# Fifth stage of a hybrid decoder step: one plain group of heads instead of two, with the second group's weight sums formed there

## The chip, the cores and the metric

The kernel is one launch on one core of a Trainium2 chip. The metric is the device time of that core in microseconds; the median of three runs of the kernel before is 2309.34 us (2308.86 to 2309.92). All data are fp32 in the device's main memory.

## The reference, cut to what matters

One step of a small decoder: a pooling mixer (layer A), one shared K/V projection, and a layer B of sliding-window attention with sinks, each closed by a layer norm. 1024 prompt tokens and 8 samples of one token pass through, so 1032 columns in all.

```python
def attn_layer(x, pos, kb, vb, k_pos, q_pos, blocked, w_in, sinks, w_out, g_ln, b_ln):
    B, T, _ = x.shape
    z = x @ w_in
    q = rope_partial(z[..., :D_ATTN].reshape(B, T, N_HEADS, HEAD_DIM), pos)
    gate = z[..., D_ATTN:]
    ...
    o = attn_core(q, kb, vb, q_pos, k_pos, sinks).reshape(B, T, D_ATTN)
    y = (o * jax.nn.silu(gate)) @ w_out
    return layer_norm(ALPHA * x + y, g_ln, b_ln)

def reference(...):
    ...
            xp, sp = pool_layer(xp, prefix_p, pos_p, w_in_a[i], ...)
            xs, ss = pool_layer(xs, state_pool[i], pos_s, w_in_a[i], ...)
            k_p, v_p = shared_kv(xp, pos_p, w_kv)
            ...
            xp = attn_layer(xp, pos_p, kb_p, vb_p, ..., w_in_b[j], sinks_b[j], w_out_b[j], ...)
            xs = attn_layer(xs, pos_s, kx_s, vx_s, ..., w_in_b[j], sinks_b[j], w_out_b[j], ...)
```

Here `x @ w_in`, `x @ w_kv` and the two `@ w_out` are the large products: 2048 deep, 2048 or 4096 wide (the K/V one 512).

## The kernel before

**Tiles.** The tokens are cut into two chunks, c = 0 with 512 columns and c = 1 with 520. Each large product is made as weights (128 by 128 blocks, held) times activations (columns stream). An fp32 operand is split into a high part (a cast, done by ScalarE) and a low part (the rest, a subtraction done by VectorE), and a product is three matmuls: high by high, high by low, low by high. A weight block set of 128 rows by 1024 columns is prepared by one load (L285, on the queue of SyncE), one cast (L505, ScalarE) and one subtraction (L520, VectorE). Activation tiles are prepared the same way by a load (L828), a cast (L838) and a subtraction (L847); `x_begin(nxt)` opens that work for the next phase, one small step with each tick of the program.

**Stages and phases.** There are eight stages: input product of layer A for c = 0 and c = 1, its output product for both, then the same for layer B: `bi` (K, V, queries, gates, attention) for c = 0, the fifth stage, and c = 1, the sixth, and `bo` (output product) for both. The tuple `PHASES` lists them. The stages that begin on fresh activations, the first and the fifth, are cut into two phases, a plain one (`PLAIN`) and one that uses a seven-product scheme.

- *Plain* (`unit`, L698): one result tile of 128 rows by 512 columns is 48 matmuls of 512 columns (16 blocks times three; L712, L713, L714) into one PSUM bank, closed by one ScalarE copy (L2127, L2135, L2140). A unit has four ticks. In the fifth stage the plain phase has `part` (0, 2): four units for K and V (two each), then for each of the two groups p four units (query and gate tiles of t = 2p and 2p + 1), twelve in all.
- *Seven-product* (`seven`, L596): a pair of result tiles is made by seven products instead of eight on halves of the token columns, 24 matmuls each of 256 (c = 1: 260) columns (L684, L685, L686), 168 in all for what 96 matmuls of 512 columns make in the plain form. It needs seven prepared weight operands instead of four plain blocks, and after each product a ScalarE or VectorE step on the bank (L623 to L657).

**Weight sums.** Four of the seven operands are sums of weight blocks. `first_pair` (L335) loads the blocks, forms the four sums on VectorE (L349) and, with `keep`, stores each of them (512 KB) by a DMA from GpSimd's queue (L351), so that the next stage's `next_pair` only loads them. Where the plain phase has used the blocks without sums (`bare_pair`), nothing is stored, and the sixth stage forms them itself with `first_pair(..., False)`. The tuple `FORM` = (0, 1) names the groups for which this is so.

**Banks.** `psD` (L242) hands out three PSUM banks in a ring, one a unit. The seven-product scheme uses the same three banks by a table of its own (L604), in which two of them change roles from pair to pair (`flip`). A product that is given a bank has to wait until the step that reads the bank's earlier content is done.

**Order.** `in_order` (L85) fixes the order of each engine's instructions as the source writes them. What an engine does next is therefore settled when the program is built: events at ticks (`at`), the small steps of `x_tick`, and a side job whose steps are taken one a tick. During the plain phase of the fifth stage the side job is the layer norm of chunk 1 (`ln_gen(1)`: VectorE L974, L1037, L1071, L895 to L898; ScalarE L1060), and the attention of the first heads runs too (VectorE L1899, L1903, L1921, L1922; ScalarE L1914, L1927).

The next phase's activations are opened inside the loop over t, for groups 0 and 1 at t = 1, between its query unit and its gate unit, five units before the end of the plain phase:

```python
                self.unit(q_done)
                if t == 2 * ps[-1] - 1:
                    self.x_begin(nxt)
                self.last = t == 2 * ps[-1] + 1
                self.unit(g_done)
```

Of the kernel before, what the change touches and what calls it, by code (L numbers as in the profile page):

```python
# [47 lines left out]
N_CST = K_MP + P + 1  # L48

PHASES = (  # L50
    ("ai", 0, (0, 1)), ("ai", 0, (1, 8)), ("ai", 1, (0, 8)), ("ao", 0, None), ("ao", 1, None), ("bi", 0, (0, 2)),
    ("bi", 0, (2, 8)), ("bi", 1, (0, 8)), ("bo", 0, None), ("bo", 1, None),
)
PHASE_OF = {"x": "ai", "g": "ao", "h": "bi", "o": "bo"}
INPUT_OF = {k: x for x, k in PHASE_OF.items()}
# [15 lines left out]
)  # L71

LATE = (2, 3)
FORM = (0, 1)
X_KEEP = 5
X_AGE = 3
SIDE_KEEP = 5
# [113 lines left out]
class Kern:  # L191
# [185 lines left out]
    def build_stream(self):  # L377
        io = self.io
        w = []
        for kind, c, part in PHASES:  # L380
# [18 lines left out]
            elif kind == "bi":  # L399
                if part[0] == 0:  # L400
                    w += self.next_pairs("wkv", range(2), locked) if seven else pr("wkv", 0) + pr("wkv", 1)
                if seven:
                    for p in range(*part):
                        for q in (p, 8 + p):
                            if c == 1 and p in FORM:
                                f = self.first_pair("wib", q, False)
# [3 lines left out]
                else:  # L410
                    for p in range(*part):
                        q, g = ((self.bare_pair if p in FORM else pr)("wib", q) for q in (p, 8 + p))
                        w += q[:2] + g[:2] + q[2:] + g[2:]
# [1700 lines left out]
    def phase_bi(self, c, ps, nxt):  # L2114
        nc = self.nc
        T = CHUNKS[c][1]
        if ps[0] == 0:
            self.kv_open(c)
        if not self.strassen:
            for done in (self.k_done, self.v_done):  # L2120
                box = {}
                for j in range(2):

                    def take(ps, j=j, done=done, box=box):
                        if j == 0:
                            box["s"] = self.mem.full(2 * T)
                        nc.scalar.copy(box["s"].a[:, j * T : (j + 1) * T], ps[:])  # L2127
                        if j == 1:
                            done(c, box["s"])

                    self.unit(take)
            for t in range(2 * ps[0], 2 * ps[-1] + 2):
                def q_done(ps, t=t):
                    s = self.mem.half(T)
                    nc.scalar.copy(s.a[:, :T], ps[:])  # L2135
                    self.q_done(c, t, s, 1, 4)

                def g_done(ps, t=t):
                    s = self.mem.half(T)
                    nc.scalar.copy(s.a[:, :T], ps[:])  # L2140
                    self.gate_done(c, t, s, 1)

                self.attend(c, t, 9, 13 if t <= 2 * ps[-1] else 8, 2)
# [5 lines that stand above are left out]
            self.last = False  # L2149
            return  # L2150
        if ps[0] == 0:
            pairs = []
            for done in (self.k_done, self.v_done):
                box, z0, z1 = self.two(T)
                pairs.append((z0, z1, lambda done=done, box=box: done(c, box["s"])))
            self.both(c, *pairs)

        def queries(p):
            t0 = 2 * p
            if T > TP and p % 4 == 3:  # L2160
                self.at(2, lambda p=p: self.dec_keys(p // 4))
            for n in range(2):
                t = t0 + n
                at, s1, ticks = (12 + 7 * n, {12: 11, 13: 9}.get(t, 12), SPREAD) if t < 14 else (
                    11 + 7 * n, {14: 10, 15: 8}[t], CLOSE
                )
                self.attend(c, t, at, s1, 2, t > 12, ticks)
            if p == ps[-1]:
                self.x_begin(nxt)
                if c == 1:  # L2170
                    self.ahead = 6, 4, 3
                else:
                    self.ahead = 8, 4, 3
                    self.at(30, lambda: setattr(self, "ahead", (7, 4, 3)))
            box, z0, z1 = self.two(T)
            self.pair(c, z0, z1, lambda t0=t0, box=box: self.q_done(c, t0, box["s"], 2, 3))

        def gates(p):
            box, z0, z1 = self.two(T)

            def done():
                self.gate_done(c, 2 * p, box["s"], 2)
                if T > TP and p % 4 == 3:
                    self.decode(c, p // 4)

            self.last = p == ps[-1]
            self.pair(c, z0, z1, done)

        for p in ps:
            queries(p)  # L2190
            gates(p)
        self.last = False
# [296 lines left out]
```

## Time and profile before

| what | value |
|---|---|
| median of three runs | 2309.34 us (2308.86 to 2309.92) |
| span of the profiled execution | 2308.8 us |
| instructions recorded | 50518 |
| TensorE's granted clock, mean | 0.999 |
| TensorE's waits for VectorE, L520 | 5.8 us in 8 |
| L349, sums of weight blocks | 136, 1222 ns each |
| stores of sums of the layer B input weights and the like | 512 KB each, GpSimd's queue |
| main-memory traffic | 463.00 MB read, 172.47 MB written, 275 GB/s |

The span is the one core's time from the first to the last instruction. Busy times of TensorE are wall time with a matmul in flight; matmuls overlap, so the mean duration of one in the group rows (283 ns for L684) is longer than the step from one to the next, which the timeline shows. In the rows below, tiles are named by the program without buffer numbers: `m` is an area of the on-chip memory, `pD` one of the PSUM banks, `sm` a small tile, `prm` the parameters. L12 is line 12 of the kernel before.

The profiled execution was 0.5 us shorter than the median.

### The profile page before, as it was taken

How to read it: one execution, taken by the hardware profiler on the slowest of the kernel's cores; microseconds unless marked ns; L12 is line 12 of the kernel's file. 1: busy time of each engine (PE TensorE's matmuls, PEld its weight loads, DVE VectorE, ACT ScalarE, POOL GpSimd, SP SyncE). 2: the span in 40 equal slices, each digit the busy share in tenths (PEclk: the TensorE clock that was granted, in tenths of full speed). 3: DMA queues.
4: the chain of work that ended last, by engine and by line, in shares of the span. 5: the costliest groups of instructions: out<-in, count | busy, mean ns of one | idle time of the engine just before them, and what ended most of it. 6: DMA issues, size and time to landing. Idle time of an engine off the chain costs nothing.

```text
span 2308.8 us, 50518 instructions
## 1 busy us (share of the span) xinstructions
PE 2286.2 (99%) x20417; PEld 2216.1 (96%) x20417; DVE 1943.5 (84%) x2415; ACT 1389.0 (60%) x2547; POOL 191.1 (8%) x359
## 2 busy tenths in 40 slices
PE   9999999999999999999999999999999999999998
PEld 7999999999999999999889999999999999999998
DVE  8888889877868878998878888999877777888997
ACT  5544446544546556555576766785776678656665
POOL 0111100010000000000001111100000000000001
PEclk9999999999999999999999999999999999999999
DMA  7879679988989989999767667777787778799894
GB/s 260 284 245 315 229 252 327 317 302 300 303 304 323 339 293 321 317 385 359 235 241 249 224 237 243 263 273 233 236 261 233 248 241 293 245 365 360 286 342 149
DMA packets 246395, 648.31 MB, mean 281 GB/s; under 512 B 25201, under 2 KB 106001, under 8 KB 246161
## 3 DMA queue, kind: packets, MB, share of 16 engines
q1 hardware_dynamic: 204288, 493.13, 63.7%
q0 software_dynamic: 41872, 151.96, 17.0%
q8 instruction: 159, 2.61, 0.5%
q14 instruction: 76, 0.61, 0.1%
HBM read 463.00 MB, written 172.47 MB: 275 GB/s over the span
## 4 chain that ended last, share of the span: by engine, by line
PE 56%; DVE 1%; DMA 1%; ACT 0%; issue 0%; POOL 0%; SPq 0%; DVEq 0%; POOLq 0%
PE pD L684 15%; PE pD L686 14%; PE pD L685 14%; PE pO L1955 2%; PE pD L712 2%; PE pD L714 2%; PE pD L713 2%; PE pS L1878 2%; PE pS L1931 1%; DMA m<-in_wob 0%; PE pS L1955 0%; PE pO L684 0%; PE pO L685 0%; PE pO L686 0%; DVE m L520 0%; DMA m<-in_wib 0%
## 5 line engine op out<-in xcount | busy, mean ns | idle before, releaser
L684 PE MATMUL pD<-m,m 128*128 128x260 f32 (+1 forms) x5088 | 1441.1, 283 | 4.4 <-ACT pD L623 2.2
L686 PE MATMUL pD<-m,m 128*128 128x260 f32 (+1 forms) x5088 | 1434.0, 282 | 5.8 <-DVE m L520 5.8
L685 PE MATMUL pD<-m,m 128*128 128x260 f32 (+1 forms) x5088 | 1434.2, 282 | 0.0
L684 PEld LDWEIGHTS pD<-m,m 128*128 128x128 f32 x5088 | 958.9, 188 | 13.7 <-issue 6.2
L686 PEld LDWEIGHTS pD<-m,m 128*128 128x128 f32 x5088 | 959.5, 189 | 7.6 <-DVE m L520 7.4
L685 PEld LDWEIGHTS pD<-m,m 128*128 128x128 f32 x5088 | 958.6, 188 | 0.5
L520 DVE TENSOR_TENSOR m<-m,m 128x1024 fp32r<-128x1024 f32 x690 | 834.1, 1219 | 94.4 <-ACT m L505 37.9
L505 ACT CAST m<-m 128x1024 fp32r<-128x1024 f32 x690 | 720.6, 1049 | 247.5 <-DVE m L349 122.4
L349 DVE TENSOR_TENSOR m<-m,m 128x1024 f32<-128x1024 f32 x136 | 166.2, 1222 | 8.6 <-DMA m<-in_wia 5.6
L847 DVE TENSOR_TENSOR m<-m,m 128x1024 fp32r<-128x1024 f32 (+1 forms) x118 | 144.0, 1225 | 7.4 <-ACT m L838 5.8
L838 ACT CAST m<-m 128x1024 fp32r<-128x1024 f32 (+1 forms) x118 | 123.3, 1051 | 8.3 <-DVE m L520 3.9
L657 ACT COPY m<-pD 128x260 f32<-128x260 f32 (+1 forms) x88 | 32.9, 374 | 125.8 <-PE pD L686 125.6
L645 DVE TENSOR_TENSOR m<-pD,m 128x260 f32<-128x260 f32 (+1 forms) x92 | 38.3, 417 | 74.3 <-ACT pD L644 68.2
L1914 ACT ACTIVATE m<-m,sm 128x128 f32<-128x128 f32 x256 | 99.4, 392 | 0.0
L623 ACT ACTIVATE pD<-pD 128x260 f32<-128x260 f32 (+1 forms) x90 | 33.3, 370 | 98.8 <-PE pD L686 98.4
L1181 PE MATMUL pD<-m,m 128*128 128x260 f32 (+1 forms) x528 | 91.5, 323 | 0.0
L712 PE MATMUL pD<-m,m 128*128 128x512 f32 x224 | 89.1, 398 | 0.0
L714 PE MATMUL pD<-m,m 128*128 128x512 f32 x224 | 88.2, 394 | 0.0
L713 PE MATMUL pD<-m,m 128*128 128x512 f32 x224 | 88.1, 393 | 0.0
L1181 PEld LDWEIGHTS pD<-m,m 128*128 128x128 f32 x528 | 79.4, 188 | 8.2
L1927 ACT ACTIVATE m<-m,sm 128x128 f32<-128x128 f32 x256 | 81.9, 391 | 7.8 <-DVE sm L1922 7.2
L632 ACT COPY m<-pD 128x260 f32<-128x260 f32 (+1 forms) x92 | 34.4, 374 | 82.6 <-PE pD L686 82.4
(257 smaller groups left out, 2102.7 us busy)
## 6 DMA issues: line engine op xcount, KB each, us to landing
m<-in_wib SPq DMA_DIRECT2D x132, 512.0 KB
m<-in_wia SPq DMA_DIRECT2D x128, 512.0 KB
m<-swoa SPq DMA_DIRECT2D x64, 512.0 KB
swia<-m POOLq DMA_DIRECT2D x56, 512.0 KB, 4.8
m<-swia SPq DMA_DIRECT2D x56, 512.0 KB
m<-swob SPq DMA_DIRECT2D x56, 512.0 KB
m<-in_wob SPq DMA_DIRECT2D x52, 512.0 KB
m<-in_woa SPq DMA_DIRECT2D x48, 512.0 KB
```

The costliest lines, as they stand in the source:

```text
L349: self.nc.vector.tensor_add(s[out].a[:, :1024], s[x].a[:, :1024], s[y].a[:, :1024])
L505: self.nc.scalar.copy(hi.r[:, :1024], self.stream[self.cast].src().a[:, :1024])
L520: self.nc.vector.tensor_sub(lo.r[:, :1024], s.src().a[:, :1024], hi.a[:, :1024])
L684: nc.tensor.matmul(ps[:, :TH], wh[:, s], h, start=new and k == 0, stop=False, skip_group_check=on)
L685: nc.tensor.matmul(ps[:, :TH], wh[:, s], l, start=False, stop=False, skip_group_check=on)
L686: nc.tensor.matmul(ps[:, :TH], wl[:, s], h, start=False, stop=k == 7, skip_group_check=on)
L712: nc.tensor.matmul(ps[:], wh[:, s], h, start=par == 0 and k == 0, stop=False)
L713: nc.tensor.matmul(ps[:], wh[:, s], l, start=False, stop=False)
L714: nc.tensor.matmul(ps[:], wl[:, s], h, start=False, stop=par == 1 and k == 7)
L838: self.nc.scalar.copy(h.r[:, :n], s.a[:, :n])
L847: self.nc.vector.tensor_sub(l.r[:, :n], s.a[:, :n], h.a[:, :n])
L1181: nc.tensor.matmul(ps[:, : cs.stop - cs.start], ws[:, s], d[:, cs], start=f0 and k == 0, stop=l0 and k == 3,)
```

## The change

The plain phase of the fifth stage keeps K, V and the first group; the second group's queries and gates are made by the seven-product phase behind it. `FORM` shrinks with it: the sums of group 1 are formed in the fifth stage by `first_pair` with `keep`, stored, and loaded in the sixth stage, which before loaded the blocks and formed them. With one group the condition in the loop over t (t = 2 * ps[-1] - 1) is never met; `x_begin(nxt)` is called ahead of the last V unit instead, five units before the end of the plain phase as before.

```diff
 PHASES = (
-    ("ai", 0, (0, 1)), ("ai", 0, (1, 8)), ("ai", 1, (0, 8)), ("ao", 0, None), ("ao", 1, None), ("bi", 0, (0, 2)),
-    ("bi", 0, (2, 8)), ("bi", 1, (0, 8)), ("bo", 0, None), ("bo", 1, None),
+    ("ai", 0, (0, 1)), ("ai", 0, (1, 8)), ("ai", 1, (0, 8)), ("ao", 0, None), ("ao", 1, None), ("bi", 0, (0, 1)),
+    ("bi", 0, (1, 8)), ("bi", 1, (0, 8)), ("bo", 0, None), ("bo", 1, None),
 )
@@
-FORM = (0, 1)
+FORM = (0,)
@@ def phase_bi, loop over K and V, j = 0, 1
+                    if len(ps) == 1 and j == 1 and done == self.v_done:
+                        self.x_begin(nxt)
                     self.unit(take)
```

Lines behind the third piece have a number that is two higher in the changed kernel (L2140 becomes L2142).

What the edit does to the order of the engines, at the three places that the prediction speaks of:

**VectorE near the end of the plain phase.** Ahead of the softmax sums (L1921) of the first heads, in the kernel before. Names: `m` areas with the slot and use number, L1071 and L895 to L898 are steps of the layer norm of chunk 1, L520 the low part of a weight block set.

```order
L520 TENSOR_TENSOR m51_1620_13756<-m33_1609_13615,m13_1615_13699 128x1024
L1071 TENSOR_TENSOR m46_1574_13292<-m46_1574_13292,m20_1549_13115 128x1040
L895 TENSOR_TENSOR m24_1625_13802<-m34_1563_13222 128x260
L896 TENSOR_TENSOR m24_1625_13802<-m34_1563_13222 128x260
L897 TENSOR_TENSOR m24_1625_13802<-m34_1563_13222,m24_1625_13802 128x260
L898 TENSOR_TENSOR m24_1625_13802<-m34_1563_13222,m24_1625_13802 128x260
L1071 TENSOR_TENSOR m43_1576_13310<-m43_1576_13310,m20_1549_13115 128x1040
L520 TENSOR_TENSOR m47_1629_13822<-m52_1613_13695,m2_1621_13758 128x1024
L1921 TENSOR_TENSOR sm_230_13742<-sm_230_13742,sm_229_13741 128x8
```

The same stretch in the changed kernel:

```order
L847 TENSOR_TENSOR m48_1633_13804<-m51_1593_13436,m7_1621_13707 128x1024
L1071 TENSOR_TENSOR m46_1574_13292<-m46_1574_13292,m20_1549_13115 128x1040
L895 TENSOR_TENSOR m19_1637_13828<-m34_1563_13222 128x260
L896 TENSOR_TENSOR m19_1637_13828<-m34_1563_13222 128x260
L897 TENSOR_TENSOR m19_1637_13828<-m34_1563_13222,m19_1637_13828 128x260
L898 TENSOR_TENSOR m19_1637_13828<-m34_1563_13222,m19_1637_13828 128x260
L847 TENSOR_TENSOR m23_1638_13838<-m25_1605_13536,m49_1634_13806 128x1024
L1071 TENSOR_TENSOR m43_1576_13310<-m43_1576_13310,m20_1549_13115 128x1040
L520 TENSOR_TENSOR m42_1643_13852<-m3_1624_13717,m53_1631_13780 128x1024
L349 TENSOR_TENSOR m21_1623_13715<-m13_1616_13629,m21_1623_13715 128x1024
L349 TENSOR_TENSOR m13_1616_13629<-m13_1616_13629,m3_1624_13717 128x1024
L1921 TENSOR_TENSOR sm_230_13764<-sm_230_13764,sm_229_13763 128x8
```

Activation subtractions (L847) and weight sums (L349) of the seven-product phase now stand between the same layer-norm steps; one more L847 stands ahead of L974, one more between L1996 and L1071, and one more L349 just ahead of the rows shown. Between the last L1048 and L1921 these are four L847 and three L349; everything else there is as before.

**ScalarE at the end of the eighth unit.** In both kernels this is the gate tile of t = 1; in the kernel before (copy L2140) four more units follow:

```order
L1060 ACTIVATE m46_1574_13292<-m46_1574_13292,prm_75 128x520 x2
L505 CAST m28_1630_13824<-m7_1619_13754 128x1024
L1060 ACTIVATE m43_1576_13310<-m43_1576_13310,prm_75 128x520 x2
L1927 ACTIVATE m10_1616_13713<-m10_1616_13713,sm_230_13742 128x128 x4
L838 CAST m49_1633_13867<-m0_1623_13782 128x1024
L2140 COPY m41_1635_13876<-pD_231_13752 128x512
L1993 ACTIVATE m17_1636_13878<-m41_1635_13876 128x512
```

In the changed kernel it is the last unit of the plain phase:

```order
L838 CAST m32_1639_13840<-m14_1622_13709 128x1024
L1060 ACTIVATE m46_1574_13292<-m46_1574_13292,prm_75 128x520 x2
L505 CAST m12_1644_13858<-m13_1616_13629 128x1024
L1060 ACTIVATE m43_1576_13310<-m43_1576_13310,prm_75 128x520 x2
L1927 ACTIVATE m24_1627_13735<-m24_1627_13735,sm_230_13764 128x128 x4
L838 CAST m40_1648_13903<-m15_1635_13808 128x1024
L2142 COPY m52_1650_13911<-pD_231_13774 128x512
```

The cast L505 ahead of the copy now reads a sum (`m13`, the last L349 of the rows above) instead of a loaded block.

**TensorE where the plain phase ends.** In the kernel before, where the twelfth unit gives way to the first product of the next phase:

```order
L712 MATMUL pD_244_14252<-m6_1537_13045,m0_1667_14119 128x512
L713 MATMUL pD_244_14252<-m35_1541_13078,m0_1667_14119 128x512
L714 MATMUL pD_244_14252<-m6_1537_13045,m3_1673_14213 128x512
L684 MATMUL pD_245_14373<-m49_1633_13867,m28_1674_14215 128x256 [waits Activation_49]
L685 MATMUL pD_245_14373<-m50_1640_13905,m28_1674_14215 128x256
```

And in the changed kernel, behind the eighth unit:

```order
L712 MATMUL pD_231_13774<-m6_1537_13045,m50_1618_13633 128x512
L713 MATMUL pD_231_13774<-m35_1541_13078,m50_1618_13633 128x512
L714 MATMUL pD_231_13774<-m6_1537_13045,m28_1625_13719 128x512
L684 MATMUL pD_232_13921<-m31_1599_13487,m26_1626_13721 128x256 [waits Activation_49]
L685 MATMUL pD_232_13921<-m0_1603_13532,m26_1626_13721 128x256
```

Counted by the ring of three, pD_244 is bank 2 and pD_245 bank 1, two different ones; after eight units instead of twelve, pD_231 is bank 1 and pD_232, by the table of the seven-product scheme, is bank 1 as well.

Over the whole program the change takes 192 matmuls of 512 columns away and adds 336 of 256 columns; ScalarE has six more casts L505 and two more of each of the six bank steps L623 to L657 that it does, VectorE six more L520 and two more L645 and L650. The number of L349 is the same (eight move from the sixth stage to the fifth); GpSimd's queue has eight more stores of 512 KB (L351), SyncE's queue six more weight loads (L285).

## The prediction

> **What bounds the kernel now.** I read the page's first part first, then the slices, then the chain that ended last.
>
> ```profile
> span 2308.8 us, 50518 instructions
> PE 2286.2 (99%) x20417; PEld 2216.1 (96%) x20417; DVE 1943.5 (84%) x2415; ACT 1389.0 (60%) x2547; POOL 191.1 (8%) x359
> PE   9999999999999999999999999999999999999998
> PE 56%; DVE 1%; DMA 1%; ACT 0%; issue 0%; POOL 0%; SPq 0%; DVEq 0%; POOLq 0%
> ```
>
> TensorE (PE) has work in flight for 99% of the span, in every slice. The next engine is VectorE (DVE) with 84%, which is close enough that a stage can be bound by it for a while. So a change pays if it takes matmul time away and nothing makes TensorE wait. The view of waits tells what does so today:
>
> ```profile
> PE pD L686 <- DVE m L520: 5.8, 8, 2.5
> PE pD L684 <- ACT pD L623: 2.2, 2, 1.3
> PE pD L684 <- ACT m L657: 1.7, 1, 1.7
> ```
>
> These are small sums over the whole span, so TensorE is hardly ever late, and by little. Next come the stretches of the fifth stage. Columns: stretch, its length, busy us and instructions of PE, PEld, DVE, ACT, POOL, granted clock, DMA share, GB/s.
>
> ```profile
> 1081.00:1121.00 40.00, 40.00 (x174) 32.35 (x173) 35.62 (x35) 17.33 (x20) 4.47 (x8) 1.00 0.70 250
> 1132.00:1169.00 37.00, 37.00 (x219) 29.70 (x219) 36.54 (x59) 28.11 (x53) 4.05 (x8) 1.00 0.91 322
> 1169.00:1217.00 48.00, 48.00 (x356) 38.63 (x355) 31.60 (x40) 29.11 (x70) 3.29 (x7) 1.00 0.59 199
> 1217.00:1506.00 289.00, 289.00 (x3259) 281.76 (x3257) 257.69 (x300) 202.63 (x474) 37.54 (x75) 1.00 0.71 245
> 1267.00:1284.00 17.00, 17.00 (x146) 17.00 (x146) 15.61 (x20) 12.89 (x33) 1.93 (x5) 1.00 0.79 268
> ```
>
> The plain part runs to 1217, the seven-product part from there to 1506. VectorE is full from 1132 to 1169 (36.54 of 37.00), because the layer norm of chunk 1 runs there as a side job; only from 1169 to 1217, during units nine to twelve, does it have air (31.60 of 48). These are the four units that the change takes out.
>
> **The change part by part.**
>
> *Matmuls.* The second group leaves the plain form: four units of 48 matmuls, 192 of 512 columns, against two pairs of 168, 336 of 256 columns. In the first stretch only the wide form runs: 40.00 / 174 = 0.230 us a step. The last stretch has only the narrow one: 17.00 / 146 = 0.1164 us. So 192 x 0.230 = 44.2 us go and 336 x 0.1164 = 39.1 us come: **-5.0 us**. (The trace may lack some records, which moves both prices alike; between -4.7 and -5.3.)
>
> *The border of the plain part.* In the kernel before, the last unit's bank and the first product's bank are different ones. With eight units they are the same, so the first L684 now waits for the copy that reads the last unit's bank (L2142, before L2140). TensorE finishes unit eight here, and begins unit nine without a wait:
>
> ```profile
> 1165.94 0.39 PE L714 MATMUL pD<-m,m 128*128 128x512 f32 x1
> 1166.17 0.40 PE L712 MATMUL pD<-m,m 128*128 128x512 f32 x1
> ```
>
> The copy is in a fixed place on ScalarE (ACT), behind work that waits for VectorE. VectorE's timeline, with the engine's last pause in front:
>
> ```profile
> 1130.33 0.70 DVE L974 TENSOR_TENSOR m<-m 128x520 f32<-128x520 f32 x1 [0.70 <-ACT m L973]
> 1135.85 1.22 DVE L520 TENSOR_TENSOR m<-m,m 128x1024 fp32r<-128x1024 f32 x1
> 1136.99 1.23 DVE L1071 TENSOR_TENSOR m<-m,m 128x1040 f32<-128x1040 f32 x1
> 1160.19 1.22 DVE L520 TENSOR_TENSOR m<-m,m 128x1024 fp32r<-128x1024 f32 x1
> 1161.42 0.17 DVE L1921 TENSOR_TENSOR sm<-sm,sm 128x8 f32<-128x8 f32 x1
> ```
>
> From the pause at 1130 on the engine is saturated, so each operation that the change puts into this stretch delays all behind it. The order shows seven more of them ahead of L1921: four L847 and three L349, each 128x1024, at 1136.99 - 1135.85 = 1.14 us a step. That is 8.0 us, less the pause of 0.70 that one L847 ahead of it can fill: L1921 comes at 1161.4 + 7.3 = 1168.7 instead of 1161.4, and the last of the sums (L349), which stands directly ahead of it, ends at about 1168.6. ScalarE's timeline of the place:
>
> ```profile
> 1162.72 1.03 ACT L505 CAST m<-m 128x1024 fp32r<-128x1024 f32 x1
> 1163.66 1.53 ACT L1060 ACTIVATE m<-m,prm 128x520 f32<-128x520 f32 x2
> 1165.10 1.27 ACT L1927 ACTIVATE m<-m,sm 128x128 f32<-128x128 f32 x4
> 1166.28 1.03 ACT L838 CAST m<-m 128x1024 fp32r<-128x1024 f32 x1
> 1167.21 0.57 ACT L2140 COPY m<-pD 128x512 f32<-128x512 f32 x1
> ```
>
> From L505 the order is the same in the changed kernel (L505, L1060, L1927, L838, the copy), but its L505 casts that last sum and cannot begin before 1168.6. From the start of L505 to the end of the copy the rows give 1167.21 + 0.57 - 1162.72 = 5.1 us, so the bank is free at 1173.7, where TensorE is ready at 1166.2: a new wait of **+7.5 us** (L684 behind L2142). All of TensorE's later work stands behind this L684, and every bank step and area that waits for TensorE comes later by as much; ScalarE and VectorE themselves go on with their backlog meanwhile. Bounds: 2.5 us if VectorE finds 5 us of the 7.3 elsewhere (a weight or activation tile that is ready sooner), 10 us if the added activation casts L838, which stand ahead of L505, push too. Without the shared bank nothing would be won for good, since the layer-norm steps and casts behind it on VectorE are just as late. The kernel before had units nine to twelve to catch up.
>
> *The clock.* A wait of this length has a price behind it. In the seventh stage there is a wait of 2.46 us, in the sixth one of 1.72:
>
> ```profile
> 1943.41 0.28 PE L686 MATMUL pD<-m,m 128*128 128x260 f32 x1
> 1945.41 0.39 PE L684 MATMUL pD<-m,m 128*128 128x256 f32 x1 [1.72 <-ACT m L657]
> 2084.59 0.27 PE L685 MATMUL pD<-m,m 128*128 128x256 f32 x1
> 2087.33 0.58 PE L686 MATMUL pD<-m,m 128*128 128x256 f32 x1 [2.46 <-DVE m L520]
> 2086.85:2090.26 3.41, 2.93 (x13) 2.93 (x14) 3.32 (x4) 2.13 (x4) 0.53 (x1) 0.50 1.04 405
> 2090.26:2093.67 3.41, 3.41 (x30) 3.41 (x30) 3.41 (x4) 2.64 (x4) 0.00 (x0) 1.00 1.05 406
> ```
>
> Behind the longer one the granted clock is 0.50 for a stretch of 3.41 us: 13 matmuls take 2.93 us, 0.225 each, where full clock would do them in 13 x 0.1164 = 1.5. That cost 1.4 us. A wait three times as long should do at least this. I bound it by nothing and by two such stretches (6.82 x 0.48 = 3.3 us) and take **+2.0**, above the measured case.
>
> The Trainium skill, "TensorE: Matmul & The Clock Gate", section "Part 1: The HAM clock gate (the "warmup" mystery)", says that the clock halves after an idle window of about 3.4 us and comes back after a busy one. The trace is harsher in the first part (2.46 us of idleness sufficed) and milder in the second (the stretch at half clock was itself not fully busy). By the page, half clock would last for a remainder of a window and one full window, 3.4 to 6.8 us, an estimate of 1.6 to 3.3 us, or 2.5 in the middle in place of my 2.0.
>
> *Other banks that meet.* The rotation is shifted for all that follows. The order shows that the meeting before the 1.72 us wait above goes away, and two others arise, early in the sixth and in the seventh stage, where the bank's copy L657 has to follow its matmuls:
>
> ```profile
> 1555.89 0.38 ACT L657 COPY m<-pD 128x260 f32<-128x260 f32 x1 [0.68 <-PE pD L686]
> ```
>
> ScalarE is idle and waits there, so such a copy starts at once: 0.38 plus some 0.3 for the two hand-overs, 0.7 each. Together -1.7 + 1.4 = **-0.3**, between -1.7 and +1.5.
>
> *Sums and stores.* The eight sums that move cost VectorE 1.22 us each:
>
> ```profile
> L349 DVE TENSOR_TENSOR m<-m,m 128x1024 f32<-128x1024 f32 x136 | 166.2, 1222 | 8.6 <-DMA m<-in_wia 5.6
> L520 DVE TENSOR_TENSOR m<-m,m 128x1024 fp32r<-128x1024 f32 x690 | 834.1, 1219 | 94.4 <-ACT m L505 37.9
> ```
>
> In the sixth stage 8 x 1.22 = 9.8 us leave VectorE. None of the waits above lies there, so nothing is won. In the fifth stage they come with six more L520, and the seven-product part has 257.69 busy of 289, 89%; one more group of the same mix keeps that share, so it is hidden by matmuls as the others are. If that cover were gone, it would be at most its start, where VectorE enters late: I take **+0.5**, between 0 and 2. The eight stores and six loads of 512 KB are 7 MB on a DMA share of 0.71 in that stretch: nothing, while the stores' areas come free in time.
>
> Sum: -5.0 + 7.5 + 2.0 - 0.3 + 0.5 = **+4.7 us** on a span of 2308.8. The median of the runs is 0.5 us above that span, and I add the sum to the median: 2309.3 + 4.7 = **2314.0 us**.
>
> **The rivals.**
>
> *A. The wait is hidden and the gain stands.* The mechanism: VectorE's added operations find room ahead of 1130, or ScalarE gets to the copy by 1166.2, and TensorE goes on at once. For it: the first stretch shows VectorE with 35.62 of 40.00, 4.4 us of air that could take operations if they stood earlier. Against it: the order puts six of the seven behind 1130.33, where the timeline has no pause. Time: 2309.3 - 5.0 - 0.3 + 0.5 = 2304.5. It decides from a wait under 0.2 us; at 2.5 us (and no loss of clock) the result is 2307.0, no change.
>
> *B. The lateness goes on.* VectorE has lost its air of 48 - 31.60 = 16.4 us, in which in the kernel before it caught up with layer norm, casts and sums; at 89% of load it recovers 0.11 us for each us. Should the first products wait for operands (L686 behind L520) for another 3 us, with the half clock for two stretches: 2309.3 - 5.0 + 10 + 3.3 - 0.3 + 3 = 2320.3. For it: eight waits of L686 for L520 are in the trace, which is how this would look. Against: while TensorE stands for 7.5 us, VectorE catches up by the same time.
>
> *C. Only the seventh stage's rush moves.* The 2.46 us wait at 2084.59 comes where VectorE and DMA are both full (3.38 of 3.41 us, DMA share 1.04) in this row:
>
> ```profile
> 2083.44:2086.85 3.41, 1.42 (x13) 1.22 (x11) 3.38 (x6) 0.68 (x1) 0.54 (x1) 1.00 1.04 401
> ```
>
> The shifted ticks may take it away (with its clock loss 2.46 + 1.4 = 3.9) or double it: 2314.0 - 3.9 = 2310.1, or 2317.9. For it: memory areas are handed out by the same order throughout. Against: the operations of that stage stay the same.
>
> **How the numbers follow.** The forecast, a wait of 6 to 9 us with a loss of clock, has a chance of 0.62; its own range is 2309.3 - 5.3 + 6 + 0 - 0.3 = 2309.7 to 2309.3 - 4.7 + 9 + 3.3 - 0.3 + 1.5 = 2318. Rival A has 0.12, B 0.18, C 0.08. A measurement of this kernel can tell about 0.2%, 4.6 us, from no change, so "no change" reaches from 2304.7 to 2313.9. The forecast's middle lies at the upper edge of that: I give 0.40 of its 0.62 to slower and 0.22 to the same. With A (0.10 faster, 0.02 same), B (slower), C (0.05 same, 0.03 slower): faster 0.10, same 0.29, slower 0.61. The range is 2305 to 2321: it leaves out the lower half of A and more than one mishap at a time.
>
> **What would show it.** In the changed profile, the wait list should have a row of PE pD L684 for ACT m L2142 of 6 to 9 us at about 1166, VectorE without a pause from 1130 to 1169, L1921 at 1168 to 1169, and a stretch behind 1173 with a granted clock near 0.50. The L712 to L714 counts fall by 64 each, and the seven-product part is about 40 us longer. The 1.72 us wait for L657 should be gone, with two of some 0.7 in its place. The prediction is wrong if L684 starts at the border without a wait (A), if waits of L686 for L520 add up to more than some 9 us in the fifth stage (B), or if the fifth stage comes out as said and the total not (C).

## The result, and the profile after

The changed kernel takes 2319.66 us (median of five runs, 2317.84 to 2321.98) against 2309.29 us before (five runs, 2306.61 to 2309.92): a ratio of 1.0046, 95% interval 1.0034 to 1.0057. It is slower by some 10 us. The forecast was 2314.0, slower, in a range of 2305 to 2321; rival B, the lateness that goes on, had been priced at 2320.3.

The profiled execution after has a span of 2319.3 us. The page, and the view of TensorE's waits (engine and tile, line, what it waited for: us in total, times, longest):

```profile
span 2319.3 us, 50898 instructions
PE 2285.4 (99%) x20561; PEld 2222.3 (96%) x20561; DVE 1950.8 (84%) x2421; ACT 1395.5 (60%) x2560; POOL 196.8 (8%) x367
```

```profile
PE pD L684 <- ACT m L2142: 7.2, 1, 7.2
PE pD L686 <- DVE m L520: 6.3, 14, 0.9
PE pD L684 <- ACT pD L623: 5.7, 3, 3.4
PE pS L1878 <- DVE m L1848: 1.8, 1, 1.8
PE pD L684 <- ACT m L657: 0.9, 2, 0.5
```

The busy shares say almost nothing: 99% as before, a busy time even 0.8 us shorter. The waits say where to look: a new one of 7.2 us for L2142, and a longer one for L623, 3.4 us where the longest was 1.3. Both lie in the fifth stage. Where that stage ends is told by the first matmul of the sixth (L672), in TensorE's timeline, before and after:

```profile
1506.61 0.62 PE L672 MATMUL pD<-m,m 128*128 128x260 f32 x3 [0.46 <-ACT m L657]
```

```profile
1517.72 0.28 PE L672 MATMUL pD<-m,m 128*128 128x260 f32 x1
```

So the fifth stage ends 11.1 us later, 0.7 of which it brought along from its start, and all the stages behind it together come out 0.6 us shorter (2319.3 - 2308.8 = 10.5). The whole loss lies in the stage that was changed. The stretches of the fifth stage after the change (length; busy us of PE, PEld, DVE, ACT, POOL; granted clock; DMA share; GB/s):

```profile
1130.00:1166.90 36.90, 36.90 (x218) 29.45 (x216) 36.52 (x52) 24.36 (x44) 3.53 (x7) 1.00 0.77 268
1166.90:1174.30 7.40, 0.17 (x1) 0.00 (x0) 7.26 (x14) 6.69 (x13) 1.97 (x4) 0.85 1.04 385
1174.32:1178.92 4.60, 4.60 (x21) 4.60 (x22) 3.37 (x5) 2.72 (x6) 0.14 (x1) 0.51 1.02 418
1228.00:1240.00 12.00, 7.73 (x49) 7.36 (x50) 9.93 (x11) 6.24 (x15) 1.07 (x2) 0.87 0.85 307
1240.00:1517.70 277.70, 277.70 (x3153) 270.84 (x3152) 243.86 (x286) 197.10 (x474) 36.01 (x72) 1.00 0.70 240
```

VectorE is full up to the border (36.52 of 36.90). Then TensorE stands still, runs 4.6 us at half clock, goes on, and stands again between 1228 and 1240. From 1240 to the end of the stage it has no idle time at all. Both places in TensorE's timeline, with ScalarE's rows at the border:

```profile
1174.32 0.58 PE L684 MATMUL pD<-m,m 128*128 128x256 f32 x1 [7.24 <-ACT m L2142]
...
1228.34 0.36 PE L684 MATMUL pD<-m,m 128*128 128x256 f32 x1 [0.41 <-DVE m L650]
...
1229.38 0.39 PE L686 MATMUL pD<-m,m 128*128 128x256 f32 x1 [0.57 <-DVE m L520]
...
1235.59 0.38 PE L684 MATMUL pD<-m,m 128*128 128x256 f32 x1 [3.36 <-ACT pD L623]
```

```profile
1155.98 0.59 ACT L2137 COPY m<-pD 128x512 f32<-128x512 f32 x1 [2.23 <-PE pD L714]
1159.53 1.05 ACT L505 CAST m<-m 128x1024 fp32r<-128x1024 f32 x1 [2.96 <-DVE m L349]
...
1169.20 1.04 ACT L505 CAST m<-m 128x1024 fp32r<-128x1024 f32 x1 [0.68 <-DVE sm L1921]
...
1173.69 0.57 ACT L2142 COPY m<-pD 128x512 f32<-128x512 f32 x1
```

The account of the stage closes: -5.0 (matmuls), +7.24 and +4.34 (0.41 + 0.57 + 3.36) of waits, +2.2 of half clock behind the first (21 matmuls in 4.60 us, which take 2.4 at 0.1164) and 1.7 behind the second (27 matmuls from 1235.59 to 1240.40, 4.81 us, which take 3.1 at 0.1164), +0.7 from its start: 11.2 against the 11.1 measured.

**The second wait.** What TensorE waits for at 1235.59 is the bank step L623, and that stood on ScalarE behind a cast that waited itself. ScalarE's and GpSimd's timelines:

```profile
1234.22 1.04 ACT L505 CAST m<-m 128x1024 fp32r<-128x1024 f32 x1 [4.87 <-DMA to<-m]
1235.17 0.37 ACT L623 ACTIVATE pD<-pD 128x256 f32<-128x256 f32 x1
```

```profile
1223.46 0.53 POOL L351 DMA_DIRECT2D swib<-m  x1 [2.45 <-DVE m L349]
1224.72 0.53 POOL L351 DMA_DIRECT2D swib<-m  x1 [0.72 <-DVE m L349]
1225.33 0.55 POOL L1967 DMA_DIRECT2D o<-m  x1
1226.79 0.53 POOL L899 DMA_DIRECT2D to<-m  x1 [0.91 <-DVE m L895]
1228.26 0.53 POOL L899 DMA_DIRECT2D th<-m  x1 [0.94 <-DVE m L650]
```

A cast that waits for a store is a matter of memory areas: its *destination* is an area that a transfer is still reading. The order of the changed program has it in two rows, GpSimd's store of sums of the attention output (`to`) and ScalarE's cast:

```
L899 DMA to0_85<-m25_1705_14527 128x1024
L505 CAST m25_1713_14578<-m24_1700_14410 128x1024 [waits DMAHW0_49,DMASW4_49]
```

Area 25 is stored at 1226.79, the store lands at 1234.2, and the cast starts at 1234.22. In the kernel before the same store is issued at 1225.75 and reads area 28. It lands 6.1 us later, at 1231.9, and the area's next use is a bank copy of ScalarE (L638) at 1232.38. What is new beside it is the last store of the layer norm of chunk 1 (`th`, 1228.26). VectorE's timeline has the layer norm's last L895, before and after:

```profile
1172.68 0.42 DVE L895 TENSOR_TENSOR m<-m 128x260 f32<-128x260 f32 x1
```

```profile
1226.30 0.42 DVE L895 TENSOR_TENSOR m<-m 128x260 f32<-128x260 f32 x1
```

In the kernel before that is well inside the plain phase, which ends at 1217; here it is 52 us behind the border wait's end.

### The profile page after: what moved, and what is told of

The parts are those of the page before. It is cut to its first block, busy times and chain, and to the rows that moved or that the text cites. A ratio compares the mean times of both kernels' runs of the same rounds, so it can differ in the third digit from the quotient of the medians.

```text
span 2319.3 us, 50898 instructions
## 1 busy us (share of the span) xinstructions
PE 2285.4 (99%) x20561; PEld 2222.3 (96%) x20561; DVE 1950.8 (84%) x2421; ACT 1395.5 (60%) x2560; POOL 196.8 (8%) x367
## 5 line engine op out<-in xcount | busy, mean ns | idle before, releaser
L684 PE MATMUL pD<-m,m 128*128 128x260 f32 (+1 forms) x5200 | 1473.8, 283 | 14.3 <-ACT m L2142 7.2
L686 PE MATMUL pD<-m,m 128*128 128x260 f32 (+1 forms) x5200 | 1466.8, 282 | 6.3 <-DVE m L520 6.3
L685 PE MATMUL pD<-m,m 128*128 128x260 f32 (+1 forms) x5200 | 1466.4, 282 | 0.0
L684 PEld LDWEIGHTS pD<-m,m 128*128 128x128 f32 x5200 | 981.0, 189 | 24.6 <-ACT m L2142 7.7
L686 PEld LDWEIGHTS pD<-m,m 128*128 128x128 f32 x5200 | 981.7, 189 | 9.2 <-DVE m L520 9.2
L685 PEld LDWEIGHTS pD<-m,m 128*128 128x128 f32 x5200 | 980.9, 189 | 0.5
L520 DVE TENSOR_TENSOR m<-m,m 128x1024 fp32r<-128x1024 f32 x696 | 841.0, 1218 | 109.7 <-ACT m L505 45.2
L505 ACT CAST m<-m 128x1024 fp32r<-128x1024 f32 x696 | 726.8, 1049 | 244.2 <-DVE m L349 116.1
L349 DVE TENSOR_TENSOR m<-m,m 128x1024 f32<-128x1024 f32 x136 | 166.1, 1222 | 9.5 <-DMA m<-in_wia 5.6
L847 DVE TENSOR_TENSOR m<-m,m 128x1024 fp32r<-128x1024 f32 (+1 forms) x118 | 143.7, 1224 | 3.4 <-ACT m L838 1.4
L657 ACT COPY m<-pD 128x260 f32<-128x260 f32 (+1 forms) x90 | 33.6, 374 | 129.3 <-PE pD L686 129.1
L645 DVE TENSOR_TENSOR m<-pD,m 128x260 f32<-128x260 f32 (+1 forms) x94 | 39.1, 416 | 80.1 <-ACT pD L644 74.3
L623 ACT ACTIVATE pD<-pD 128x260 f32<-128x260 f32 (+1 forms) x92 | 34.0, 370 | 104.7 <-PE pD L686 104.5
L1181 PE MATMUL pD<-m,m 128*128 128x260 f32 (+1 forms) x528 | 91.5, 323 | 0.0
L1181 PEld LDWEIGHTS pD<-m,m 128*128 128x128 f32 x528 | 79.4, 188 | 8.2
L632 ACT COPY m<-pD 128x260 f32<-128x260 f32 (+1 forms) x94 | 35.2, 374 | 83.8 <-PE pD L686 83.5
L644 ACT COPY pD<-pD 128x256 f32<-128x256 f32 (+1 forms) x80 | 28.9, 361 | 85.0 <-PE pD L686 84.9
L629 ACT COPY m<-pD 128x260 f32<-128x260 f32 (+1 forms) x92 | 34.0, 369 | 59.4 <-PE pD L686 52.6
L1112 DVE TENSOR_TENSOR m<-m 128x512 f32<-128x512 f32 (+5 forms) x80 | 55.5, 693 | 11.5 <-ACT m L1096 10.0
```

What stands on the lines that cost most here:

```text
L349: self.nc.vector.tensor_add(s[out].a[:, :1024], s[x].a[:, :1024], s[y].a[:, :1024])
L505: self.nc.scalar.copy(hi.r[:, :1024], self.stream[self.cast].src().a[:, :1024])
L520: self.nc.vector.tensor_sub(lo.r[:, :1024], s.src().a[:, :1024], hi.a[:, :1024])
L684: nc.tensor.matmul(ps[:, :TH], wh[:, s], h, start=new and k == 0, stop=False, skip_group_check=on)
L685: nc.tensor.matmul(ps[:, :TH], wh[:, s], l, start=False, stop=False, skip_group_check=on)
L686: nc.tensor.matmul(ps[:, :TH], wl[:, s], h, start=False, stop=k == 7, skip_group_check=on)
```

## The experiments

**1. Undo the shared bank.** Two roles of the bank table are swapped for the fifth stage and swapped back behind it:

```diff
             self.last = False
+            self.flip = 1 - self.flip
             return
@@
+        if c == 1:
+            self.flip = 1 - self.flip
         if ps[0] == 0:
             self.kv_open(c)
```

> The changed kernel with the two PSUM banks of the seven-product table swapped for the fifth stage, so that its first product no longer gets the bank of the last plain unit. Theory (VectorE is late, the bank only shows it): the 7.2 us wait for L2142 at 1167 goes, but TensorE runs two or three products (2.8 us each) and then waits for L847 or L520, which VectorE cannot bring sooner; 0 to 3 us won at 1240, total 2316 to 2320. Rival (the shared bank is the whole cause): the wait and its half clock, 9 us, are won and stay won, total about 2310.5.

Ratio to the kernel before 1.0063 (1.0046 to 1.0079), median 2323.07: above its forecast of 2316 to 2320, and no better than the change itself, where the theory still allowed a small gain. The wait for the copy is gone, and these have come in its place:

```profile
1175.52 2.39 PE L1878 MATMUL pS<-m,m 64*32 64x160 f32 x64 [3.93 <-DVE m L1848]
...
1194.41 0.39 PE L684 MATMUL pD<-m,m 128*128 128x256 f32 x1 [3.50 <-ACT pD L644]
...
1519.58 0.40 PE L672 MATMUL pD<-m,m 128*128 128x260 f32 x2
```

TensorE runs on past the border and then waits twice for the same late engines, first in the attention scores. The 3.2 us at 1233 stays. The stage ends 1.9 us later than with the shared bank, where the matmuls show three restarts at half clock instead of two. In this order the bank shows the lateness; it doesn't cause it.

**2. The swap in the kernel before.** The same three lines in the kernel before were meant to make the banks meet there.

> The kernel before with the same swap of two banks, so that its first product does meet the bank of the twelfth unit. Theory (the size of the border wait is VectorE's lateness, which units nine to twelve have taken up by then): a wait of 1 us or less at 1217, total 2309 to 2311. Rival (a meeting of banks costs some 7 us wherever it lies, with half clock behind it): total about 2318.

They don't: the twelfth unit has bank 2, and the swap gave the first product bank 0. Ratio 1.0002 (0.9992 to 1.0011), no wait at 1217. It tells only that the swap itself costs nothing. The proper test turns the ring by two at the start of the plain phase (`self.ring = (self.ring + 2) % 3`), which gives both bank 1:

> The kernel before with the ring of banks turned by two at the start of the plain phase, so that the twelfth unit and the first product really share bank 1 (the earlier swap of two banks gave the product bank 0, where the twelfth unit has bank 2). Theory (the wait is as long as ScalarE and VectorE are late): the copy of the twelfth unit ends at 1219.2 in the kernel before and TensorE is there at 1217.35, so a wait of about 1.9 us for L2140 without a loss of clock; total 2310 to 2312. Rival (a meeting of banks costs 7 us and half clock wherever it lies): about 2318.

```profile
PE pD L684 <- ACT m L2141: 1.7, 1, 1.7
```

1.7 us, without loss of clock; ratio 1.0014 (1.0005 to 1.0024), median 2312.93, just above the forecast of 2310 to 2312. The fifth stage of the profiled run ends 1.4 us later than before, at 1508.03; the rest of the loss lies in the seventh stage. A meeting of banks costs what the other engines are late at that place: 1.7 us behind the twelfth unit, 7.2 behind the eighth.

**3. End the layer norm inside the plain phase.** Four more of its steps are forced there:

```diff
+                for k in (24, 26, 28, 30):
+                    self.at(k, lambda: self.side and self.lastO < self.i - 1 and self.side_step())
                 self.every, self.room = 1, -20
```

> The changed kernel with four more steps of the layer norm of chunk 1 forced into the plain phase, so that it ends there as in the kernel before. Theory (the second wait, 3.4 us at 1232, is a cast that is given a memory area whose store has not landed, since the end of the layer norm keeps areas away from the seven-product phase): that wait and its half clock go, -5 us; the border wait grows by the VectorE time of the two tails that now stand ahead of it, 0 to 3.3 us; total 2315 to 2318. Rival (VectorE simply has too much to do in the stage): the waits only move, total 2319 to 2321.

```profile
PE pD L684 <- ACT m L2142: 11.4, 1, 11.4
PE pD L686 <- DVE m L520: 5.6, 11, 0.9
PE pD L684 <- ACT pD L623: 2.2, 2, 1.3
```

The wait at 1232 is gone, with the two small ones before it, and the border wait is 4.1 us longer, where 0 to 3.3 was expected. Its stage ends at 1514.1, 3.6 us earlier than the change's; the ratio is 1.0038 (1.0023 to 1.0053), which its interval can't tell from the change's 1.0046. So the cause of the second wait is as read, while the work, put back ahead of the border, is paid there.

**4. No stores of group 1's sums.** `first_pair` keeps none of them for this group, and the sixth stage forms them again (`FORM` = (0, 1)).

> The changed kernel without the eight stores of group 1's sums in the fifth stage; the sixth stage forms them again, eight L349 more and eight loads as before. Theory: the stores have no part in it; the border wait stays at 7.2 us and the wait at 1232 stays within 1 us, total 2318 to 2321. Rival (the added stores delay the ones that hold the areas): the wait at 1232 goes with its half clock, total about 2314.5.

Border wait 7.3 us; the wait at 1232 fell to 2.0 us, outside what the theory allowed but not gone; ratio 1.004 (1.0025 to 1.0055), which its interval can't tell from the change's. ScalarE's timeline:

```profile
1230.73 1.04 ACT L505 CAST m<-m 128x1024 fp32r<-128x1024 f32 x1 [3.79 <-DMA to<-m]
```

The cast still waits for the store of `to`, so the second wait needs none of the added stores. That store took 6.3 us from its issue to landing, where with the added stores it took 7.4, and the two small waits at 1228 and 1229 are gone. The fifth stage of this run ends at 1513.8, 3.9 us earlier than the change's, but from there to the end, with the sums formed in the sixth stage, it takes 804.2 us instead of 801.6. So the stores have a part in the size of the second wait, but leaving them out did not make the kernel faster. Why the store of `to` landed sooner was not tested.

**5. Take work off VectorE.** The layer norm's multiplication for chunk 1 works on 32 of 520 columns:

```diff
-                nc.vector.tensor_mul(t, t, b2(rr))
+                if c == 1 and self.ph == "bi0":
+                    nc.vector.tensor_mul(t[:, :, :32], t[:, :, :32], b2(rr)[:, :, :32])
```

> The changed kernel with the layer norm's multiplication by the standard deviation for chunk 1 (L1071, eight of 128x1040) done on 32 of 520 columns only, so VectorE has some 8 us less to do in the plain part, seven of them ahead of L1921, and nothing else moves in the order. Theory: the border wait falls by as much, from 7.2 us to 1 or less, and its half clock goes; the wait at 1232 stays, at 2 to 3.4 us; total 2310 to 2313. Rival (bank, ScalarE or the transfers set the border wait): it stays over 4 us, total over 2315.

This theory fell. 8 us less for VectorE made the border wait 6.1 instead of 7.2 us, and the ratio is 1.0045 (1.003 to 1.006), median 2320.28 where 2310 to 2313 was expected. VectorE's timeline shows where the rest went:

```profile
1146.03 0.69 DVE L1999 SCALAR_TENSOR_TENSOR m<-m,m 128x512 f32<-128x512 f32 x1 [3.88 <-ACT m L1996]
...
1152.46 1.33 DVE L1902 COPY_PREDICATED m<-cst,pS 128x1024 f32<-128x1024 int32 x1 [0.76 <-issue]
...
1167.78 0.16 DVE L1924 TENSOR_TENSOR sm<-sm,sm 128x8 f32<-128x8 f32 x1
```

(L1924 here is L1921 before.) VectorE gets ahead and then waits 3.88 us for ScalarE, which waits for TensorE's sixth unit. Relief ahead of that point is lost. The same with the layer norm's end inside the plain phase and L1031 narrowed too, 16 us off VectorE:

> As e2_ln_in, with L1071 and the subtraction of the mean L1031 for chunk 1 on 32 of 520 columns: VectorE has some 16 us less to do in the plain part and the layer norm still ends there. Theory: neither the border wait nor the one at 1232; the gain in matmul time is left alone, -5 us, total 2303 to 2306. Rival (the gain in matmul time is not there, or is eaten later in the sixth to eighth stage): total 2308 to 2311.

```profile
PE pD L684 <- ACT m L2145: 9.8, 1, 9.8
```

9.8 instead of 11.4, no wait at 1232, ratio 1.0032 (1.0021 to 1.0044), median 2317.53 where 2303 to 2306 was expected. VectorE's load in the plain part as a whole isn't what sets the border wait.

**6. Give work to GpSimd.** As 3, with L895 to L898 of chunk 1's layer norm on GpSimd.

> As e2_ln_in, with the four subtractions and additions that follow each layer-norm pair of chunk 1 (L895 to L898, 128x260 each, 32 in all, 13.5 us of VectorE) done by GpSimd. Theory (VectorE's lateness): both waits go if GpSimd keeps up, total 2304 to 2308, better than the kernel before. Rival (GpSimd is slow, or it slows VectorE by working beside it, or holds its own queue of stores): the border wait stays over 4 us, total 2314 or more.

The rival holds: a border wait of 16.5 us, ratio 1.0064 (1.0048 to 1.0081), median 2324.4. It had named three reasons; the rows show the second, that VectorE slows down, and don't exclude the others. Two groups of VectorE, in this run and in that of experiment 3, between 1130 and the border wait's end:

```profile
L1072 DVE TENSOR_TENSOR m<-m,m 128x1040 f32<-128x1040 f32 x8 | 13.0, 1643 | 0.0
...
L349 DVE TENSOR_TENSOR m<-m,m 128x1024 f32<-128x1024 f32 x3 | 5.2, 1744 | 0.0
```

```profile
L1071 DVE TENSOR_TENSOR m<-m,m 128x1040 f32<-128x1040 f32 x8 | 9.8, 1233 | 0.0
...
L349 DVE TENSOR_TENSOR m<-m,m 128x1024 f32<-128x1024 f32 x3 | 3.7, 1220 | 0.0
```

On average these operations of VectorE take a third to two fifths longer where GpSimd works beside it.

**7. Leave the first sums out.** The seven operands of the first pair are loaded as plain blocks, so three L349 are not in the last one and a half units; group 1's sums are formed in the sixth stage.

```diff
+                if kind == "bi":
+                    raw = lambda q: [self.lone(self.quads("wib", q)[k]) for k in (0, 3, 2, 1, 0, 2, 3)]
+                    pr = lambda name, q, pr=pr: raw(q) if q == 1 else pr(name, q)
```

> The changed kernel with the four sums of the first pair of the seven-product phase left out (its seven operands are loaded as plain blocks), so that three L349 and the casts that wait for them leave the last one and a half units of the plain phase; the sixth stage forms group 1's sums again. Theory (the border wait is the length of the one list that VectorE and ScalarE work through in turns from the end of the seventh unit at 1156 to the copy L2142): it falls by those three operations and more, from 7.2 us to 2 to 4; the wait at 1232 stays; total 2313 to 2316. Rival (the list is set before 1150 and the sums lie beside it): the border wait stays over 6 us, total over 2318.

```profile
PE pD L687 <- ACT pD L626: 8.9, 5, 5.0
PE pD L689 <- DVE m L523: 5.3, 12, 0.9
PE pD L687 <- ACT m L2145: 2.8, 1, 2.8
```

The border wait fell to 2.8 us as the theory said: 3.4 us of sums were worth 4.4 us, where 8 us of layer norm were worth 1.1. The total did not follow: ratio 1.0043 (1.0028 to 1.0058), median 2319.37, outside its forecast. Three waits of 0.4 to 1.3 us behind the border and one of 5.0 at 1233 (L626, before L623) took most of it.

**8. A better order.** Layer-norm steps forced early, at ticks 6, 8, 10 and 12, where VectorE still has air (experiment 8a); that with the banks of experiment 1 and weight loads one operand sooner, `(6, 4, 3)` for `(5, 4, 3)` (8b); and 8a's steps in the kernel before (8c).

> The changed kernel with only the four layer-norm steps forced early (ticks 6 to 12). Theory: the wait at 1232 goes as in e2_ln_in, while the border wait grows less than there since the added steps lie ahead of the last units; border wait 7 to 9 us, total 2313 to 2317. Rival (where in the plain phase the steps lie does not matter): border wait 11 us and total 2318 as in e2_ln_in.

> The changed kernel with three edits of order: the banks swapped as in e1_bank, four more steps of the layer norm of chunk 1 forced early in the plain phase (ticks 6 to 12, where VectorE still has air), and weight loads one operand sooner there. Theory: no wait at 1232, waits of 3 to 8 us in two or three places behind the border that VectorE's list still makes; total 2310 to 2315, not better than the kernel before. Rival (the order alone was at fault and the gain in matmul time can be had): total under 2307.

> The kernel before with the same four layer-norm steps forced early. Theory: it has no wait in the fifth stage that this could take away; total within 3 us of the kernel before, 2306 to 2312. Rival (an earlier layer norm helps wherever it is): more than 4 us faster.

8a: border wait 7.6 us, none at 1232, stage end 1513.9, ratio 1.0041 (1.0027 to 1.0055), median 2317.24, just outside what was expected. The border wait is nearly the change's own here, so it was not the longer one of experiment 3 that took the second wait away. 8b is the best form of the change that was found:

```profile
PE pS L1878 <- DVE m L1848: 4.5, 2, 3.8
PE pD L684 <- ACT pD L623: 3.1, 3, 1.3
```

Ratio 1.0024 (1.0014 to 1.0035), median 2314.51: faster than the change, still slower than the kernel before, with its largest wait (3.8 us) again for VectorE behind the border. Which of its edits won the 2.7 us against 8a was not separated. 8c came out slower than the kernel before, 1.0019 (1.001 to 1.0028), median 2313.17 and outside its forecast too: the fifth stage had nothing to win, and a wait for L657 in the seventh grew to 2.8 us. No version was found that beats the kernel before.

## Why the prediction was right, and where it was short

The direction and the largest new wait came as forecast. The size did not: the forecast's own sum reached 2318 at most, and the median of 2319.66 lies in the range of 2305 to 2321 only because that was drawn wider. That it lies so near the 2320.3 of rival B is luck, since B's mechanism did not come.

- **Matmuls, -5.0.** The row for it is the account of the stage, which closes within 0.2 us with this term. It was not measured alone; every version that was to show it bare (5, 8b) kept a wait.
- **The border wait, 7.5.** 7.24 measured, by the path foretold: L1921 was to come at 1168.7 and came at 1169.0, the copy was to end at 1173.7 and ended at 1174.3, and TensorE was ready at 1166.9 instead of 1166.2, since the stage began 0.7 us later. The reason given was too coarse. "From the pause at 1130 on the engine is saturated, so each operation that the change puts into this stretch delays all behind it" holds in the trace, but experiment 5 shows that without the saturation the wait stays: ScalarE is tied to TensorE's units at 1143 and 1156, and from 1156 to the copy at 1173.7 the two engines work through one list in turns (cast behind sum, subtraction behind cast), 17.7 us beside a unit whose 48 matmuls take 11.1. In the kernel before this piece, from the same copy at 1155.24 to that of the eighth unit at 1167.21, took 12.0 us. Experiment 7 takes three sums out of the list, and the wait falls by more than their time.
- **"Without the shared bank nothing would be won for good".** Experiment 1 bears it out for the order of the change. It is not shown for every order: in 8b, with the banks of experiment 1 and other steps moved too, the waits at the border and just behind it add up to 4.6 us, where 8a has 7.6.
- **The clock, +2.0.** 2.2 us behind the border wait. The Trainium skill, "TensorE: Matmul & The Clock Gate", section "Part 1: The HAM clock gate (the "warmup" mystery)", has windows of about 3.4 us, from which the prediction estimated 3.4 to 6.8 us of half rate and 1.6 to 3.3 us of loss. The row (4.60 us near half clock) agrees with that estimate.
- **Other banks, -0.3.** The wait of 1.72 us before the seventh stage's first product is gone and two of 0.5 for L657 have come, as said. The 2.46 us wait at 2084 vanished, which was rival C's first case, priced there at 3.9 us. That TensorE would then wait 1.8 us for L1848 at 1950 was not seen. The stages behind the fifth came out 0.6 us shorter in all.
- **"Sums and stores", +0.5.** This is the step that failed. "Nothing, while the stores' areas come free in time" was its condition, and just that is what broke: a cast had to wait for a store of the attention output, with the layer norm's rest as the cause. Where the layer norm ends inside the plain part, this wait and the two small ones before it are gone (experiments 3 and 8a); without the sums' own stores the long one shrinks to 2.0 us and stays (experiment 4). The term measured 4.3 us of waits, 3.4 of them for that store, and 1.7 of half clock, 6.0 in place of 0.5. These 5.5 us are nearly all of the 5.8 us between the 4.7 us of the sum and the 10.5 of the profiles. Rival B had the size right and the place nearly, but named the wrong wait: it looked for L686 behind L520, of which 0.6 us came.
- **"About 40 us longer".** The seven-product part takes 343.4 us from 1174.32 to 1517.72, where it took 289.3 from 1217.35: 54 us more. Besides its 39.1 us of matmuls, the waits and half clock behind the border account for 8, and some 7 are attention matmuls. They ran between the four units before, which took 51.2 us from 1166.17 to 1217.35 with 44.2 us of plain matmuls. This moves work from one part to the other and leaves the sum as it is.

How the layer norm's leftover steps could be missed: the rows of the order that were read ended at the border. How far the side job had come there, and how many areas were free behind it, was to be had from the same order.

## What to carry to other kernels

When a phase with slack is shortened, count what its last stretch still has to finish, side jobs and their stores among it, and follow the leftovers into the next phase: there they hold memory, and a cast can wait for a store that has nothing to do with it. Where two engines feed each other in a fixed order, work costs by its place in their common list, not by an engine's load; taking load off elsewhere buys idle time. A shared buffer that shows up as the releaser of a wait may only mark an engine that is late anyway: swap the buffer first and see whether the wait moves.

## What the runs showed of the hardware

The loss of clock does not begin at one length of idleness. In the run with the ring turned by two (TensorE's timeline, then the stretch behind it with its granted clock as the third number from the end), 1.93 us in the seventh stage are followed by a clock of 0.62; at the border of experiment 7, in the same two views, 2.77 us by one of 1.00:

```profile
2090.15 0.38 PE L686 MATMUL pD<-m,m 128*128 128x256 f32 x1 [1.93 <-DVE m L520]
```

```profile
2090.20:2094.60 4.40, 4.40 (x25) 4.40 (x26) 4.31 (x4) 2.48 (x4) 0.53 (x1) 0.62 1.03 409
```

```profile
1168.52 0.39 PE L687 MATMUL pD<-m,m 128*128 128x256 f32 x1 [2.77 <-ACT m L2145]
```

```profile
1168.50:1172.00 3.50, 3.48 (x29) 3.48 (x30) 3.46 (x6) 0.63 (x1) 0.53 (x1) 1.00 1.02 375
```

The Trainium skill, "TensorE: Matmul & The Clock Gate", section "Part 1: The HAM clock gate (the "warmup" mystery)", speaks of an idle window of about 3.4 us; the first run is against that as a lower bound.

VectorE's operations with two inputs slowed from 1220 to 1744 ns on average where GpSimd did element-wise work (L349, experiment 6). Within that run, L520 took 1.22 us at 1133.63, before GpSimd's first operation at 1136.94, and 1.78 us at 1137.07. The Trainium skill, "GPSIMD Engine Reference", section "1. Specifications", says that the two engines share an interface to the on-chip memory and contend where a VectorE instruction has two inputs there; the trace agrees. GpSimd's own 128x260 operations took 872 to 1292 ns on average, where VectorE takes some 420.
